# A decoder layer on one core: the gating unit's steps spread out and its operands made a step ahead, product operands built in three steps, and down-projection chunks of 5, 14, 5, 14 and 6 k-tiles

## The chip, the cores and the metric

The kernel runs on one core of a Trainium2 chip. The metric is the device time of one execution in microseconds (us). Before the change three runs took 2702.42 to 2703.47 us, with a median of 2703.02 us. Shorter is better.

## The reference

One layer of a hybrid decoder, in float32, for 512 prompt tokens and 8 sample tokens that share the weights (2048 model columns):

```python
xn = rmsnorm(x)
q, k, v, gu, gv = split(xn @ w_in)
attn = window_attention(norm(q), norm(k), v)        # window 128, sinks, ALiBi
gu = gelu(gu); gv = layernorm(gelu(gv))
sgu = gu * (tril(W_s[group]) @ gv + b[group])       # in chunks of 128 tokens
gA, gB = sigmoid(xn @ w_gate + b_gate)
x += (gA * (attn @ w_br_attn) + gB * (sgu @ w_br_gm)) @ w_out
h = conv3(rmsnorm(x) @ w_up)
x += (silu(h_gate) * h_up) @ w_down                 # 5632 = 44 x 128 inner columns
x += sigmoid(rmsnorm(x) @ w_ple_gate) * (p @ w_ple_proj)
```

It returns x, the new keys and values, the last normalised gv rows (`gp_o`, `gs_o`) and the convolution's state.

## The kernel before, in words

**The products.** Activations lie transposed, 128 columns of the model by 520 tokens in a tile. Every operand is split into a high and a low part, and a product is made of three matmuls: high by high, high by low, low by high. A *plain* product (`ntile`, `mm`, lines 364 to 384) runs over the k-tiles of one output tile n; each k-tile takes six matmuls of 260 columns, two halves of the tokens by three. A *seven-product* pair (`wpair`, line 395) makes two output tiles of two k-tiles at a time from seven products instead of eight (Strassen's scheme in Winograd's form), each of three matmuls of 260 columns. Its parts come out of four PSUM banks a, b, c, d by copies on ACT (`snap`) and by sums on DVE (`c11`, `c22`, `c12`). The seven-product form serves the gates, the up-projection and the odd chunks of the down-projection.

**The weights.** They stream from DRAM in blocks of eight 128x128 tiles. At each block's start (`block_start`, line 292) SP starts a load, ACT casts the high part of the block two ahead (`hi`, line 279), and DVE takes the rest (`lo`, line 286). Work that was put off to a block (`at_block`) is placed there as well: "snap" before the cast, "act" and "dve" between the cast and the rest, "end" behind both.

**Who sets the order.** The order on each engine is that in which the code issues its instructions, and each engine works in that order. Side work is written as generators. `ntile` and `wpair` call `next(self.fine)` once for each k-tile, and whatever the generator does up to its next `yield` is issued there; `finish_fine` issues what is left.

**The gating unit** (`gmlp`, line 1249) is such side work, under the attention branch's projection "bra" (`branch_attn`, line 730): 16 output tiles of eight k-tiles, so 128 calls. `paced` (line 736) lets three calls pass for each step of `gmlp`. The steps, in order:

1. Load the small weights, and make the masked `whl`.
2. For each of the four token groups c, one step with eight PE transposes into two PSUM banks (`g`, line 1294) and the statistics (`stats`, DVE and a power on POOL), and one step with eight normalising writes on DVE (line 1298). All `aux` tiles share four banks.
3. For each of eight column slices d, three steps: multiply by the norm's weight (line 1310), start the `gp_o` write from POOL, and split into `gnh` (ACT, line 490) and `gnl` (DVE, line 491); two calls of the generator later the mix on PE (`mx`, lines 1320 and 1321) and its sums on DVE (lines 1327 to 1330); then one more step.
4. For the samples: eight transposes, statistics, two normalised tiles `gn` and four small diagonals `dgs` (line 1344), two steps of pause, and 16 tiny matmuls `gx` (line 1351).

The 16 gelus on which all this rests (line 1256) are issued on ACT just ahead of the first step.

**The operands of the seven products** (`woperands`, line 440) are made as side work too. For each product p of a pair of k-tiles, `begin` issues the operand's own sums on DVE (none for P1, P2, P7 and P3, one for P5 and P4, two for P6) and at once the ACT cast `X` (line 462); `end`, one round later, issues the rest on DVE (line 465). `build` paces the rounds, by `every` calls each. It serves the plain gates (P5, P6, P4 and P7 of eight pairs), the output projection and "pproj" (`w_out`, line 1360; pproj is 16 output tiles of two k-tiles, each evicted by ACT at line 1427 and written to DRAM by a transfer that ACT itself starts, line 1428), and the even chunks of the down-projection.

**The down-projection** (`ffn_down`, line 1552) takes the 44 inner k-tiles in chunks of 6, 14, 6, 12 and 6 (`FF_CHUNKS`, line 49). Chunks 0 and 2 are plain; under them the operands of the next chunk are loaded from DRAM (`fr`, line 1540) and built, with one or two calls to a round by turns. Chunks 1 and 3 are made in the seven-product form; the plain operands of the chunk behind are split under their last pairs (`f_parts`). Each result but the last chunk's is added to `x1d` in DRAM by a transfer that POOL starts (line 1558). Chunk 4 is plain and adds on DVE (`down_last`).

## Time and profile before

| | before |
|---|---|
| median of 3 runs | 2703.02 us |
| the profiled execution's own time | 2702.04 us |
| its span, first to last instruction | 2700.3 us |
| PE busy | 2673.4 us (99%), 22212 matmuls |
| DVE busy | 1871.6 us (69%) |
| ACT busy | 1287.4 us (48%) |
| POOL busy | 288.4 us (11%) |
| mean granted TensorE clock | 0.998 |
| DMA moved | 438.06 MB, mean 162 GB/s |

The profile is of one execution. Engines are PE (matmuls; PEld its weight loads), DVE (VectorE), ACT (ScalarE), POOL (GpSimd) and SP, which here only starts transfers. A group of instructions is named output <- inputs, after the tiles in the code. The view of the waits gives, for each engine and line, what ended the wait, the total in us, how often, and the longest. The timeline gives start, length and, in brackets, the idle time before an instruction and its releaser. The table by stretches gives the busy time of each engine in each stretch, the granted clock and the share of time in which the 16 DMA engines were busy. A busy PE is not yet a PE at its full clock.

### The profile page before, as it was taken

The numbers are of one execution on the slowest core, as the hardware profiler recorded it, in microseconds if no ns is written. First come the engines' busy times: TensorE is split into PE (matmuls) and PEld (weight loads), VectorE is DVE, ScalarE is ACT, GpSimd is POOL, SyncE is SP. The second block draws the span as 40 slices with busy tenths as digits, with TensorE's granted clock in tenths as the row PEclk, the third lists the DMA queues.
The fourth block names the chain that finished last, engine by engine and source line by source line (L and its number), as shares of the span: only waits on it lengthen the run. The fifth ranks groups of instructions, "written<-read, shape, count | busy, mean of one in ns | idle before, by whom it ended". The sixth has DMA issues, their size and how long they took to land.

```text
span 2700.3 us, 53713 instructions
## 1 busy us (share of the span) xinstructions
PE 2673.4 (99%) x22212; PEld 2668.0 (99%) x22212; DVE 1871.6 (69%) x2791; ACT 1287.4 (48%) x2173; POOL 288.4 (11%) x443
## 2 busy tenths in 40 slices
PE   9999999999999999999999999999999999999999
PEld 9999998999999999999999999999999999999999
DVE  6666557567666533688888888888888676576533
ACT  5365452354444233555555555555556445444321
POOL 0111001000010000011111111111111111110000
PEclk9999999999999999999999999999999999999999
DMA  5223323567667444566666666666668677675333
GB/s 188 93 81 102 103 79 122 184 206 204 190 188 239 158 134 142 193 186 171 163 177 174 162 174 174 162 177 171 166 167 249 152 180 204 153 178 183 125 132 106
DMA packets 151797, 438.06 MB, mean 162 GB/s; under 512 B 17200, under 2 KB 18352, under 8 KB 151552
## 3 DMA queue, kind: packets, MB, share of 16 engines
q1 hardware_dynamic: 117504, 337.58, 37.1%
q0 software_dynamic: 29440, 88.53, 18.8%
q10 hardware_dynamic: 4608, 8.52, 0.8%
q8 instruction: 174, 2.85, 0.4%
q14 instruction: 71, 0.58, 0.1%
HBM read 373.23 MB, written 61.33 MB: 161 GB/s over the span
## 4 chain that ended last, share of the span: by engine, by line
PE 96%; DVE 2%; ACT 1%; issue 0%; DMA 0%; POOL 0%; ACTq 0%; SPq 0%; DVEq 0%; POOLq 0%
PE wa L433 22%; PE wb L433 15%; PE mm L372 14%; PE mm L376 14%; PE mm L374 14%; PE wd L433 7%; PE wc L433 7%; PE po L1106 1%; PE s L1043 1%; ACT hi L279 0%; PE pt L1088 0%; PE pl L1654 0%; DVE lo L286 0%; DVE z L1298 0%; ACT z L1256 0%
## 5 line engine op out<-in xcount | busy, mean ns | idle before, releaser
L286 DVE TENSOR_TENSOR lo<-st,hi 128x1024 fp32r<-128x1024 f32 (+3 forms) x352 | 421.9, 1198 | 268.9 <-ACT hi L279 261.3
L433 PE MATMUL wa<-X,hi 128*128 128x260 f32 x3152 | 576.6, 283 | 0.9 <-ACT pp L1427 0.9
L433 PEld LDWEIGHTS wa<-X,hi 128*128 128x128 f32 x3152 | 485.5, 188 | 1.1 <-ACT pp L1427 1.1
L279 ACT CAST hi<-st 128x1024 fp32r<-128x1024 f32 (+3 forms) x352 | 362.3, 1029 | 195.8 <-DMA st<-in_w 83.8
L433 PE MATMUL wa<-X,lo 128*128 128x260 f32 x1576 | 444.7, 282 | 0.0
L433 PE MATMUL wb<-X,hi 128*128 128x260 f32 x2032 | 371.5, 283 | 0.0
L279 ACT CAST hi<-S 128x1024 fp32r<-128x1024 f32 (+2 forms) x219 | 222.6, 1017 | 230.0 <-DVE S L312 171.7
L286 DVE TENSOR_TENSOR lo<-S,hi 128x1024 fp32r<-128x1024 f32 (+2 forms) x219 | 258.5, 1180 | 99.9 <-ACT hi L279 99.6
L433 PEld LDWEIGHTS wb<-X,hi 128*128 128x128 f32 x2032 | 312.8, 188 | 0.0
L433 PEld LDWEIGHTS wa<-X,lo 128*128 128x128 f32 x1576 | 296.7, 188 | 0.0
L433 PE MATMUL wb<-X,lo 128*128 128x260 f32 x1016 | 286.7, 282 | 0.0
L286 DVE TENSOR_TENSOR lo<-L,hi 128x1024 fp32r<-128x1024 f32 (+2 forms) x146 | 172.5, 1181 | 125.0 <-ACT hi L279 124.6
L372 PE MATMUL mm<-xn,hi 128*128 128x260 f32 x1088 | 222.9, 286 | 5.3 <-ACT hi L279 5.3
L376 PE MATMUL mm<-xn,lo 128*128 128x260 f32 x1088 | 219.6, 283 | 0.0
L374 PE MATMUL mm<-xn,hi 128*128 128x260 f32 x1088 | 219.3, 283 | 0.0
L279 ACT CAST hi<-L 128x1024 fp32r<-128x1024 f32 (+2 forms) x146 | 148.4, 1016 | 121.3 <-PE wd L433 118.8
L433 PE MATMUL wd<-X,hi 128*128 128x260 f32 x1120 | 205.1, 283 | 0.0
L310 POOL DMA_DIRECT2D L<-in_w x73 | 63.3, 867 | 1265.5 <-issue 828.9
L433 PEld LDWEIGHTS wb<-X,lo 128*128 128x128 f32 x1016 | 191.4, 188 | 0.0
L372 PEld LDWEIGHTS mm<-xn,hi 128*128 128x128 f32 x1088 | 168.4, 190 | 5.4 <-ACT hi L279 5.3
L433 PEld LDWEIGHTS wd<-X,hi 128*128 128x128 f32 x1120 | 172.2, 188 | 0.1
L376 PEld LDWEIGHTS mm<-xn,lo 128*128 128x128 f32 x1088 | 168.8, 189 | 0.0
(313 smaller groups left out, 5966.8 us busy)
## 6 DMA issues: line engine op xcount, KB each, us to landing
st<-in_w SPq DMA_DIRECT2D x317, 512.0 KB, 4.4
S<-in_w SPq DMA_DIRECT2D x57, 512.0 KB, 3.5
S<-in_w POOLq DMA_DIRECT2D x57, 512.0 KB, 7.9
L<-in_w SPq DMA_DIRECT2D x57, 512.0 KB, 4.0
L<-in_w POOLq DMA_DIRECT2D x57, 512.0 KB, 5.6
fd<-hb SPq DMA_DIRECT2D x44, 260.0 KB, 2.2
fr<-fd SPq DMA_DIRECT2D x44, 260.0 KB, 4.9
xr<-in_x SPq DMA_DIRECT2D x32, 260.0 KB, 4.2
```

Of the source, the lines that this page charges most:

```text
L279: self.nc.scalar.copy(self.hi[v][:, c], self.st[WS.src[v]][:, c])
L286: self.nc.vector.tensor_sub(self.lo[v][:, c], self.st[WS.src[v]][:, c], self.hi[v][:, c].bitcast(F32))
L310: self.nc.gpsimd.dma_start(self.st[kind, r][:, c], self.a["w"][src][:, c], accum_op=ALU.add)
L372: mm(ps[:, h, 0:HW], lhsT=whi, rhs=xh[h], start=start, stop=False)
L374: mm(ps[:, h, 0:HW], lhsT=whi, rhs=xl[h], start=False, stop=False)
L376: mm(ps[:, h, 0:HW], lhsT=wlo, rhs=xh[h], start=False, stop=stop)
L433: nc.tensor.matmul(ps(z), lhsT=w, rhs=x, start=new and i == 0 and q == 0, stop=i == len(X[p]) - 1 and q == 2, skip_group_check=True)
L1043: nc.tensor.matmul(out, lhsT=self.cols(q, c), rhs=keys(kk, c), start=n == 0, stop=n == 1)
L1106: nc.tensor.matmul(po[:, kb * 128:kb * 128 + w], lhsT=vv[:, kb * 128:(kb + 1) * 128], rhs=pp[:, o:o + w], start=kb == 0 and n == 0, stop=k ...
```

## The change

There are four edits.

- **Gating unit.** `paced` lets four calls pass for each step instead of three. Slice d's multiplication, `gp_o` write and split become `parts(d)`, its mix and sums `mix(d, h, l)`. `parts(d + 1)` is issued one step ahead of `mix(d)`, and a slice takes two steps instead of three. The samples' transposes and statistics go from behind the slices to ahead of them: the transposes stand in one step with `parts(0)`, the normalised tiles and `dgs` in the next. `gx` stays last.
- **Operands in three steps.** `steps` replaces `begin` and `end`: a round issues the rests of the items two rounds old (`lo`, DVE), the casts of those one round old (`hi`, ACT), and the own sums of the new ones (`own`, DVE).
- **The sum of bank d** leaves `c12` and becomes `c21`, which is issued with `c22` at the start of product P3's block, ahead of that block's `lo`.
- **Chunks** of 5, 14, 5, 14 and 6 k-tiles; the operands of chunks 1 and 3 are built in rounds of 1, 1, 1 and 2 calls.

```diff
-FF_CHUNKS = (6, 14, 6, 12, 6)
+FF_CHUNKS = (5, 14, 5, 14, 6)
...
+        def c21():
+            nc.vector.tensor_sub(part("c2", 0), ps("d"), part("un", 1))
+
         def c12():
             nc.vector.tensor_add(part("c1", 1), ps("b"), part("un", 0))
-            nc.vector.tensor_sub(part("c2", 0), ps("d"), part("un", 1))
...
-                 "P6": [("snap", lambda: snap("a", "un", 0))], "P7": [("snap", lambda: snap("a", "un", 1)), ("dve", c22)],
+                 "P6": [("snap", lambda: snap("a", "un", 0))], "P7": [("snap", lambda: snap("a", "un", 1)), ("dve", c22), ("dve", c21)],
...
+            def own():
+                nonlocal src
+                if p == "P5":
+                    src = self.slot(name="tau")[:, 0:HW]
+                    nc.vector.tensor_sub(src, b11, b12)
...
+            def hi():
+                nonlocal x
+                x = self.slot(F32R, "X")
+                nc.scalar.copy(x[:, 0:HW], src)
+
+            def lo():
                 nc.vector.tensor_sub(x[:, HW:NT], src, x[:, 0:HW].bitcast(F32))
                 X[p][i] = x
...
+            hi, lo = [], []
+            while items or hi or lo:
                 for _ in range(every if isinstance(every, int) else next(every)):
                     yield
-                now, items = items[:group], items[group:]
-                new = [begin(*x) for x in now]
-                for e in ends:
-                    e()
-                ends = new
+                for f in lo:
+                    f()
+                for f, _ in hi:
+                    f()
+                lo = [f for _, f in hi]
+                new = [steps(*x) for x in items[:group]]
+                items = items[group:]
+                for f, _, _ in new:
+                    f()
+                hi = [f[1:] for f in new]
...
             for _ in g3:
-                yield
-                yield
-                yield
+                yield from [None] * 4
...
+        hl = parts(0)
+        yield
         g = [self.slot(name="gn") for _ in range(2)]
...
+        for d in range(KG):
+            new = parts(d + 1) if d + 1 < KG else None
+            yield
+            mix(d, *hl)
+            hl = new
+            yield
...
-                    X, self.fine = self.down_operands(ch[c + 1], cycle((1, 2)))
+                    X, self.fine = self.down_operands(ch[c + 1], cycle((1, 1, 1, 2)))
```

On DVE in the gating unit, behind the last normalising write of the fourth group (`z` from `g`), there stands before the first slice (its product with the norm's weight `nw`, and `gnl`), then a weight block's `lo` and the first slice's sums:

```order
L1298 TENSOR_SCALAR z_3625<-g_571_5382,sm_5394,sm_5398 128x128
L1310 TENSOR_TENSOR z_1265<-z_1265,nw_5134 128x2x256
L491 TENSOR_TENSOR gnl_5457<-z_1265,gnh_5456 128x520
L286 TENSOR_TENSOR lo_5491<-st_5416,hi_5490 128x1024
L1327 TENSOR_TENSOR mx_5516<-mx_5506,bb 128x256
```

At the same place there stands now:

```order
L1307 TENSOR_SCALAR z_3625<-g_573_5434,sm_5446,sm_5450 128x128
L1319 TENSOR_TENSOR z_1265<-z_1265,nw_5134 128x2x256
L502 TENSOR_TENSOR gnl_5531<-z_1265,gnh_5530 128x520
L286 TENSOR_TENSOR lo_5559<-st_5474,hi_5558 128x1024
L1290 BN_STATS sm_5570<-g_580_5518 8x6
L1290 BN_STATS sm_5570<-g_581_5519 8x6
L1292 BN_AGGR sm_5573<-sm_5570 8x2
L1294 TENSOR_SCALAR sm_5575<-sm_5573 8x1
L1351 TENSOR_SCALAR gn_5568<-g_580_5518,sm_5573,sm_5577 8x512
L1353 TENSOR_TENSOR gn_5568<-gn_5568,nw_5134 8x512
L1351 TENSOR_SCALAR gn_5569<-g_581_5519,sm_5573,sm_5577 8x512
L1353 TENSOR_TENSOR gn_5569<-gn_5569,nw_5135 8x512
```

The samples' chain (which goes on with `dgs`) has come between the first slice's operand and its sums; the second slice's operand follows it, ahead of the first slice's sums.

On ACT in pproj, around the fourth and fifth evictions and a block's cast (`hi`), there stands before:

```order
L462 CAST X_13558<-tau_13556 128x260
L1427 COPY pp_13567<-mm_13549 128x520
L1428 DMA ppd_146<-pp_13567 128x520
L279 CAST hi_13571<-st_13489 128x1024
L462 CAST X_13583<-tau_13581 128x260
L1427 COPY pp_13592<-mm_13570 128x520
L1428 DMA ppd_147<-pp_13592 128x520
```

and now:

```order
L468 CAST X_13554<-xb_13463 128x260
L1444 COPY pp_13564<-mm_13546 128x520
L1445 DMA ppd_146<-pp_13564 128x520
L279 CAST hi_13568<-st_13489 128x1024
L468 CAST X_13579<-tau_13556 128x260
L1444 COPY pp_13589<-mm_13567 128x520
L1445 DMA ppd_147<-pp_13589 128x520
```

Each cast `X` stands one tile later than before, so that the cast behind this `hi` reads `tau_13556`, which DVE makes a round earlier, and no longer `tau_13581`.

On DVE at the end of chunk 3, the sums of banks a, d and b (`wa`, `wd`, `wb`) of the last pair stood before in this order around the weight blocks' `lo`:

```order
L414 SCALAR_TENSOR_TENSOR c_1949_29807<-wa_29635,sn_29662 128x260
L286 TENSOR_TENSOR lo_29805<-st_29773,hi_29804 128x1024
L418 TENSOR_TENSOR c_1946_29752<-wb_29661,un_29718 128x260
L419 TENSOR_TENSOR c_1949_29807<-wd_29746,un_29718 128x260
L286 TENSOR_TENSOR lo_29850<-st_29801,hi_29849 128x1024
```

and now:

```order
L414 SCALAR_TENSOR_TENSOR c_1953_29774<-wa_29585,sn_29620 128x260
L418 TENSOR_TENSOR c_1953_29774<-wd_29711,un_29680 128x260
L286 TENSOR_TENSOR lo_29772<-st_29741,hi_29771 128x1024
L421 TENSOR_TENSOR c_1952_29717<-wb_29619,un_29680 128x260
L286 TENSOR_TENSOR lo_29820<-st_29768,hi_29819 128x1024
```

The sum of bank d has moved one `lo` ahead.

## The prediction

> **What bounds the kernel now.** I read the profile's page first, then the waits of PE, then the timeline and the table by stretches at each place where PE waits. The page:

> ```profile
> span 2700.3 us, 53713 instructions
> ...
> PE 2673.4 (99%) x22212; PEld 2668.0 (99%) x22212; DVE 1871.6 (69%) x2791; ACT 1287.4 (48%) x2173; POOL 288.4 (11%) x443
> ...
> PE 96%; DVE 2%; ACT 1%; issue 0%; DMA 0%; POOL 0%; ACTq 0%; SPq 0%; DVEq 0%; POOLq 0%
> ```

> PE is the bound nearly throughout: the chain that ended last runs on it for 96% of the span. So only three things shorten the kernel: fewer matmuls, fewer waits of PE, and less time at a lowered clock. The view of PE's waits, of which these are the rows that bear on the change:

> ```profile
> PE mx L1320 <- ACT gnh L490: 3.7, 1, 3.7
> PE mm L372 <- ACT pp L1427: 2.6, 3, 1.4
> PE gx L1351 <- DVE dgs L1344: 2.2, 1, 2.2
> PE g L1294 <- DVE z L1298: 2.0, 3, 0.8
> PE mm L372 <- DVE c L418: 1.5, 2, 0.9
> ...
> PE wa L433 <- ACT pp L1427: 0.9, 1, 0.9
> ...
> PE mx L1321 <- DVE gnl L491: 0.6, 2, 0.4
> ```

> The gating unit (mx, gx, g) holds 3.7 + 0.6 + 2.2 + 2.0 = 8.5 us, pproj (pp) 3.5 us, the ends of chunks 1 and 3 (c) 1.5 us. Two of the gating unit's waits cost more than they last, as the table by short stretches shows (the granted clock stands before the last two numbers):

> ```profile
> 429.40:430.00 0.60, 0.25 (x2) 0.18 (x2) 0.37 (x1) 0.20 (x2) 0.00 (x0) 0.93 0.26 89
> 430.00:430.60 0.60, 0.60 (x4) 0.60 (x5) 0.00 (x0) 0.60 (x1) 0.00 (x0) 0.50 0.40 149
> 433.00:433.60 0.60, 0.60 (x5) 0.60 (x5) 0.56 (x3) 0.00 (x0) 0.00 (x0) 0.72 0.47 123
> 494.80:495.40 0.60, 0.60 (x5) 0.60 (x4) 0.60 (x1) 0.00 (x0) 0.00 (x0) 0.50 0.07 14
> 501.40:502.00 0.60, 0.60 (x6) 0.60 (x6) 0.00 (x0) 0.00 (x0) 0.00 (x0) 0.83 1.03 392
> ```

> From 430.0 on PE is busy in these rows, but at half its clock. The mixed rows give the ends: 0.93 leaves 0.14 of 0.6 us at half, so it began at 429.9, and 0.72 and 0.83 end it at 433.3 and 501.6. So it lasts from 429.9 to 433.3 us behind the wait of mx, and from 494.8 to 501.6 us in and behind gx.

> **The change part by part.**

> *Chunks.* Two k-tiles go from plain to seven-product chunks. Plain they take 2 x 16 output tiles x 6 = 192 matmuls, in pairs 8 x 7 x 3 = 168: 24 fewer. The chain prices them:

> ```profile
> 605.18 2.89 PE wa L433 x24
> ```

> So 24 matmuls are 2.9 us, all on the path, and **2.9 us** go. The work of DVE and ACT on the weights grows a little in chunk 3 (blocks of seven tiles for six). Its cover is PE's product, 21 x 0.12 = 2.5 us for 2.2; chunk 1 has these blocks already, without a wait inside it. If that failed, each late block would show as a wait on lo.

> *Gating unit.* Of what PE waits for here, DVE is late:

> ```profile
> 404.87 1.29 DVE L1281 BATCH_NORM_STATS2 sm<-g 128x6 f32<-128x512 f32 x2
> 421.80 1.29 DVE L1281 BATCH_NORM_STATS2 sm<-g 128x6 f32<-128x512 f32 x2
> 427.70 0.68 DVE L1310 TENSOR_TENSOR z<-z,nw 128x512 f32<-128x512 f32 x1
> 429.07 0.70 DVE L491 TENSOR_TENSOR gnl<-z,gnh 128x520 fp32r<-128x520 f32 x1 [0.69 <-ACT gnh L490]
> 431.01 1.23 DVE L286 TENSOR_TENSOR lo<-st,hi 128x1024 fp32r<-128x1024 f32 x1 [1.24 <-ACT hi L279]
> 432.15 0.42 DVE L1327 TENSOR_TENSOR mx<-mx,bb 128x256 f32<-128x256 f32 x1
> 434.46 0.69 DVE L1310 TENSOR_TENSOR z<-z,nw 128x512 f32<-128x512 f32 x1
> 488.60 1.28 DVE L1281 BATCH_NORM_STATS2 sm<-g 8x6 f32<-8x512 f32 x2
> 493.90 0.61 DVE L1344 TENSOR_SCALAR dgs<-ident,cvt 8x8 f32<-8x8 f32 x4
> ```

> A token group takes DVE 427.70 - 421.80 = 5.9 us, one block's lo included. An operand (multiply, cast, rest) takes 429.77 - 427.70 = 2.1 us, a slice's sums 434.46 - 432.15 = 2.3 us, the samples' chain 494.5 - 488.6 = 5.9 us. PE's side:

> ```profile
> 397.40 1.03 PE L1294 MATMUL g<-ident,z 128*128 128x128 f32 x8
> 438.76 0.28 PE L1320 MATMUL mx<-whl,gnh 128*128 128x256 f32 x1
> 439.63 0.45 PE L372 MATMUL mm<-ah,hi 128*128 128x260 f32 x2
> 266.95 1.85 PE L1172 MATMUL sT<-qe,kT 128*128 128x8 f32 x16
> 494.26 3.09 PE L1351 MATMUL gx<-dgs,gn 8*128 8x8 f32 x16 [2.24 <-DVE dgs L1344]
> ```

> A call is one k-tile, 6 x 0.12 = 0.72 us; a mix adds 439.63 - 438.76 = 0.9 us, and I take 0.9 for eight transposes too. Before, a group gets six calls and its transposes, 5.2 us, against DVE's 5.9, and the first slice's mix comes six calls after its operand is issued. So PE runs into DVE three times at g and once at mx. After, a group gets eight calls, 6.7 us.

> I walk the new order with these times, from DVE's first statistics at 404.87, which the gelus ahead hold, not the pace. Four groups end at 404.87 + 4 x 5.9 = 428.5, and the first operand at 430.6. PE comes to the first mix at call 49; call 4 was at 397.4, so 45 x 0.72 + 5 x 0.9 later, at 434.3: 3.7 us to spare. The second operand now stands behind a lo and the samples' chain: 430.6 + 1.2 + 5.9 + 2.1 = 439.8, against the second mix at 434.3 + 8 x 0.72 + 0.9 = 441.0: 1.2 us to spare. From there a slice costs DVE 1.2 + 2.3 + 2.1 = 5.6 us and PE 6.7, so the margin grows. The banks for the third group's transposes are free at 404.87 + 5.9 = 410.8, and PE comes at 397.4 + 17 x 0.72 + 2 x 0.9 = 411.4: 0.6 us, the smallest margin. gx comes at call 109 of 128, its inputs long done.

> So 8.5 us of waits go. With them goes the half clock: (433.3 - 429.9) / 2 = 1.7 us, and (501.6 - 494.8) / 2 = 3.4 us. Together **13.6 us**. For gx I lean on sT: 16 products as narrow took 1.85 us at full clock, so narrow products alone did not lower it there. From above, six restarts of PE at 0.1 to 0.2 us each could go as well (14.6). From below, the half clock at gx stays and margins of 0.6 and 1.2 us become waits (8.5).

> [...]

> The gp_o writes move one step earlier on POOL, behind which only the small power of a statistics step waits; POOL is 11% busy. gnh's cast now stands on ACT ahead of an eviction of bra that has 5.8 us, and two operand pairs are alive instead of one, so a cast may wait for the mix two slices back, which PE passes 2.9 us earlier. I cost both at nothing; failing that, PE would wait at mm for its eviction.

> *Operands in three steps.* ACT no longer stops for DVE's own sums. Where PE does not wait (plain gates, output projection, chunks 0 and 2) that is worth nothing, since PE's work covers it. In pproj it is worth something, for there ACT is the slowest:

> ```profile
> 1129.38 1.05 ACT L279 CAST hi<-st 128x1024 fp32r<-128x1024 f32 x1 [0.40 <-ACT pp L1427]
> 1132.05 0.41 ACT L462 CAST X<-tau 128x260 fp32r<-128x260 f32 x1 [1.63 <-DVE tau L451]
> 1132.37 0.59 ACT L1427 COPY pp<-mm 128x520 f32<-128x520 f32 x1
> ```

> The stop of 1.63 us shrinks to some 0.3, since tau was made a round ahead. Against it, the last round of the builder before pproj is one longer: two casts, 2 x 0.32 = 0.65 us, now stand ahead of the first eviction. Net **0.7 us** of the 3.5. Bounds: all 3.5 go, or 1.3 us are added (two casts more, and the writes to DRAM set the pace anyway).

> *Bank d's sum.* Each pair's c21 lies ahead of a lo that is needed two blocks (5.8 us) later, so its 0.4 us cost nothing. PE waits for bank b's sum at the ends of chunks 1 and 3, and that still stands behind a lo. Only chunk 3's longer last block helps: 0.36 us later. I take **0.3 us** of 1.5; bounds all of it, or 0.8 more.

> *Chunks 0 and 2* get shorter, from 96 to 80 calls, 69.1 to 57.6 us. A build of seven pairs is 63 rounds, 79 calls with the first: it just fits.

> ```profile
> 2050.00:2100.00 50.00, 50.00 (x419) 50.00 (x418) 38.67 (x80) 30.25 (x66) 10.93 (x13) 1.00 0.98 247
> st<-in_w SPq DMA_DIRECT2D x8, 512.0 KB, 5.1
> x1d<-dn POOLq DMA_DIRECT2D x13, 260.0 KB, 5.7
> fr<-fd SPq DMA_DIRECT2D x12, 260.0 KB, 5.8
> ```

> In chunk 0 DVE is 77% and ACT 61% busy. The operands' work, packed into 57 instead of 61 us, brings DVE to some 83%. The DMA engines are at 0.98 already. Landing times still leave room: fr is asked for 11 to 14 calls (8 to 10 us) ahead and lands in 5.8, st has two blocks (11.5 us) for 5.1. I cost it at nothing, with 4.3 us for each chunk as the upper bound (a build that keeps its 61.9 us); the 2050 row is the nearest.

> **The sum.** 13.6 + 2.9 + 0.7 + 0.3 = 17.5 us. The profiled execution took 2702.04 us, its span and 1.7 us around it; that gives 2684.5. The median was 1.0 us above that execution, so I forecast 2685.5 us.

> **The rivals.**

> *The plain chunks are held by their operands.* For it: DMA at 0.98, and rounds 1.25 calls apart. Against: no wait of PE there before, and landing times half of what is allowed. Price: up to 4.3 us in each, so 2690 to 2694. [...]

> *The gating unit's waits move more than they go.* For it: margins of 0.6 and 1.2 us, and a chain of 5.9 us put ahead of the second slice. Against: DVE needs less than PE in each step from then on. If half of 13.6 stays: 2692.

> *Slower.* Each tile of a plain chunk still takes what its six k-tiles took, 4.3 us instead of 3.6, since evictions, accumulating writes and operands behind one another are what paces it: 16 x 0.72 = 11.5 us for each chunk, 23.0 for both, against 17.5 gained: 2708.5. It decides once both chunks lose more than 8.8 us each, half the gain. Against it: landing times did not climb at 0.98.

> *It does not do what it says:* DVE's lateness comes from the gelus alone, and all of the gating unit's loss stays under other names. Then 3.9 us go: 2699.1.

> **How the numbers follow.** Forecast 0.74, operands late 0.10, waits half kept 0.09, slower 0.04, no effect 0.03. 0.2%, about what a measurement of this kernel can tell from no change, is 5.4 us. Faster by more: 0.74 + 0.10 + 0.09 = 0.93; same 0.03; slower 0.04. Range: the low end takes the gating unit at 14.6 and most of pproj's 3.5 (2682); the high end reaches over the first two rivals (2694).

> **What would show it.** Right: no wait at mx, gx or g over 0.5 us, a granted clock of 1.00 from 400 to 510 us, PE's count lower by 24, pproj's wait near 2.8 us, no wait of PE in chunks 0 and 2. Wrong: a wait at the second slice's mx, a clock of 0.5 behind gx, waits of PE on fl, lo or X at the start of chunks 1 and 3, or on dn in the plain chunks.

## The result, and the profile after

Four runs of the changed kernel took 2683.59 to 2685.71 us, with a median of 2684.86 us, against 2702.97 us for the kernel before beside them: 18.1 us less, a ratio of 0.9933 (95% interval 0.9915 to 0.995). The forecast was 2685.5 us. The profiled execution took 2685.71 us; its span is 2684.0 us, 16.3 us less than before. The total was met; two of its four terms, the chunks by themselves and the sum of bank d, were not. The page of the kernel after:

```profile
span 2684.0 us, 53655 instructions
...
PE 2665.3 (99%) x22188; PEld 2659.5 (99%) x22188; DVE 1879.6 (70%) x2796; ACT 1287.7 (48%) x2174; POOL 288.2 (11%) x443
```

PE has 24 matmuls fewer, 22188. Its waits, from the view of the waits of the kernel after:

```profile
PE mm L372 <- ACT hi L279: 5.9, 2, 5.4
PE mm L372 <- ACT pp L1444: 2.1, 4, 0.8
...
PE wa L435 <- ACT pp L1444: 0.9, 1, 0.9
...
PE wc L435 <- DVE lo L286: 0.6, 1, 0.6
PE mm L372 <- ACT dn L1598: 0.5, 1, 0.5
...
PE mm L372 <- ACT ae L755: 0.4, 1, 0.4
```

No wait at mx, gx or g is left, and none on c at the ends of chunks 1 and 3. pproj (pp) still holds 2.1 + 0.9 = 3.0 us of its 3.5. Two waits are new: 0.5 us for an eviction of the plain chunks (dn), and 0.4 us for one of bra (ae), which stands on ACT behind the second slice's cast of gnh.

In the gating unit, the timeline of the kernel after (start, length, and in brackets the idle time ahead):

```profile
406.19 1.29 DVE L1290 BATCH_NORM_STATS2 sm<-g 128x6 f32<-128x512 f32 x2
431.21 0.70 DVE L502 TENSOR_TENSOR gnl<-z,gnh 128x520 fp32r<-128x520 f32 x1 [0.69 <-ACT gnh L501]
435.51 0.28 PE L1329 MATMUL mx<-whl,gnh 128*128 128x256 f32 x1
441.50 0.70 DVE L502 TENSOR_TENSOR gnl<-z,gnh 128x520 fp32r<-128x520 f32 x1 [0.69 <-ACT gnh L501]
442.83 0.28 PE L1329 MATMUL mx<-whl,gnh 128*128 128x256 f32 x1
487.60 1.95 PE L1368 MATMUL gx<-dgs,gn 8*128 8x8 f32 x16
```

The first statistics came at 406.19 and not at 404.87, since this execution's whole stage began 1.3 us later. With that shift the walk of the prediction gives 431.9 for the first operand's end and 435.6 for the first mix; the rows show 431.9 and 435.51. The second operand ends at 442.2, 1.1 us later than walked, for a mix at 442.83: 0.6 us to spare, where 1.2 was forecast. gx runs at full clock, 1.95 us for 3.09. But a stretch at half clock follows it, as the table by short stretches shows (granted clock before the last two numbers):

```profile
489.40:490.00 0.60, 0.60 (x6) 0.58 (x6) 0.60 (x2) 0.00 (x0) 0.00 (x0) 0.93 0.00 0
490.00:490.60 0.60, 0.60 (x5) 0.60 (x5) 0.57 (x2) 0.00 (x0) 0.00 (x0) 0.50 1.48 150
...
493.00:493.60 0.60, 0.60 (x5) 0.60 (x5) 0.00 (x0) 0.17 (x1) 0.00 (x0) 0.72 1.03 388
```

By its mixed rows it lasts from 489.9 to 493.3 us and costs 1.7.

Where the 16.3 us between the two traces come from, by starts of the same instructions in both:

| stretch | before, us | after, us | less, us |
|---|---|---|---|
| start of the span to the branch projection | 393.4 | 394.8 | -1.4 |
| branch projection (first to last k-step) | 121.2 | 109.4 | 11.8 |
| gates | 423.9 | 423.8 | 0.1 |
| output projection | 182.9 | 183.8 | -0.9 |
| pproj and the norm behind it | 57.8 | 57.5 | 0.3 |
| up-projection | 859.7 | 857.3 | 2.4 |
| chunks 0 to 4 | 471.6 | 467.2 | 4.4 |
| the rest | 189.8 | 190.2 | -0.4 |

Three rows were not in the forecast: 1.4 us lost at the start, 0.9 in the output projection, and 2.4 gained in the up-projection, whose instructions the change touches only in the place of one sum.

### The profile page after: what moved, and what is told of

Read it like the earlier page. It is cut to its first block, busy times and chain, and to the rows that moved or that the text cites. A ratio compares the mean times of both kernels' runs of the same rounds, so it can differ in the third digit from the quotient of the medians.

```text
span 2684.0 us, 53655 instructions
## 1 busy us (share of the span) xinstructions
PE 2665.3 (99%) x22188; PEld 2659.5 (99%) x22188; DVE 1879.6 (70%) x2796; ACT 1287.7 (48%) x2174; POOL 288.2 (11%) x443
## 4 chain that ended last, share of the span: by engine, by line
PE 94%; DVE 2%; ACT 1%; DMA 1%; issue 1%; POOL 0%; SPq 0%; ACTq 0%; DVEq 0%; POOLq 0%
PE wa L435 22%; PE wb L435 15%; PE mm L372 13%; PE mm L376 13%; PE mm L374 13%; PE wd L435 8%; PE wc L435 8%; DMA st<-in_w 1%; PE po L1115 1%; PE s L1052 1%; DMA ppd<-pp 0%; ACT hi L279 0%; PE pt L1097 0%; PE pl L1671 0%; DVE z L1307 0%
## 5 line engine op out<-in xcount | busy, mean ns | idle before, releaser
L286 DVE TENSOR_TENSOR lo<-st,hi 128x1024 fp32r<-128x1024 f32 (+2 forms) x348 | 419.1, 1204 | 255.5 <-ACT hi L279 252.3
L435 PE MATMUL wa<-X,hi 128*128 128x260 f32 x3200 | 582.7, 283 | 0.9 <-ACT pp L1444 0.9
L279 ACT CAST hi<-st 128x1024 fp32r<-128x1024 f32 (+2 forms) x348 | 360.3, 1035 | 204.4 <-DMA st<-in_w 91.2
L279 ACT CAST hi<-S 128x1024 fp32r<-128x1024 f32 (+1 forms) x219 | 225.3, 1029 | 233.6 <-DVE S L312 173.6
L286 DVE TENSOR_TENSOR lo<-S,hi 128x1024 fp32r<-128x1024 f32 (+1 forms) x219 | 261.8, 1195 | 90.8 <-ACT hi L279 89.5
L286 DVE TENSOR_TENSOR lo<-L,hi 128x1024 fp32r<-128x1024 f32 (+1 forms) x146 | 174.6, 1196 | 123.4 <-ACT hi L279 118.2
L372 PE MATMUL mm<-xn,hi 128*128 128x260 f32 x1088 | 223.2, 286 | 5.9 <-ACT hi L279 5.9
L279 ACT CAST hi<-L 128x1024 fp32r<-128x1024 f32 (+1 forms) x146 | 150.0, 1027 | 121.2 <-PE wd L435 120.8
L372 PEld LDWEIGHTS mm<-xn,hi 128*128 128x128 f32 x1088 | 168.3, 189 | 6.2 <-ACT hi L279 6.1
L435 PE MATMUL wc<-X,hi 128*128 128x260 f32 x928 | 169.9, 284 | 0.0
## 6 DMA issues: line engine op xcount, KB each, us to landing
st<-in_w SPq DMA_DIRECT2D x313, 512.0 KB, 4.5
S<-in_w SPq DMA_DIRECT2D x57, 512.0 KB, 3.5
S<-in_w POOLq DMA_DIRECT2D x57, 512.0 KB, 7.8
L<-in_w SPq DMA_DIRECT2D x57, 512.0 KB, 4.0
L<-in_w POOLq DMA_DIRECT2D x57, 512.0 KB, 5.5
```

The lines of the kernel that those rows point to most:

```text
L279: self.nc.scalar.copy(self.hi[v][:, c], self.st[WS.src[v]][:, c])
L286: self.nc.vector.tensor_sub(self.lo[v][:, c], self.st[WS.src[v]][:, c], self.hi[v][:, c].bitcast(F32))
L372: mm(ps[:, h, 0:HW], lhsT=whi, rhs=xh[h], start=start, stop=False)
L435: nc.tensor.matmul(ps(z), lhsT=w, rhs=x, start=new and i == 0 and q == 0, stop=i == len(X[p]) - 1 and q == 2, skip_group_check=True)
```

## The experiments

**Each edit by itself.** The kernel before with only the gating unit's edits, `parts`, `mix` and the samples' chain as in the change:

```diff
-                yield
-                yield
-                yield
+                yield from [None] * 4
...
+        for d in range(KG):
+            new = parts(d + 1) if d + 1 < KG else None
+            yield
+            mix(d, *hl)
+            hl = new
+            yield
```

> The kernel before with only the gating unit's edits (four calls to a step, operands a step ahead, samples' chain early). The sum's term: 13.6 us less, so 2689.4 us against 2703.0, with no wait of PE at mx, gx or g over 0.5 us. The rival, read from the two traces: the branch stage runs 393.44 to 514.6 us before and 394.8 to 504.2 after, 11.8 us less, because one 3.4 us stretch at half clock (490.0 to 493.3) still follows gx: 2691.2, and executions with and without that stretch 1.7 us apart. If the gating unit's waits only moved, 2696 or more.

Measured: 2689.66 us against 2703.26, a ratio of 0.9951 (0.9939 to 0.9963): 13.6 us less, the sum's term. Its profile has no wait at mx, gx or g and no stretch at half clock in the branch stage, which took 107.8 us for the 121.2 before.

With only the operands in three steps (`own`, `hi`, `lo`):

```diff
-        def begin(p, i):
+        def steps(p, i):
...
-            return end
+            return own, hi, lo
```

> The kernel before with only the operands made in three steps. The sum's term: pproj's waits (2.6 + 0.9 us) fall by 0.7, so 2702.3 us against 2703.0. First rival: the output projection, which took 0.9 us longer in the trace of after than of before (first to last k-step of its products 183.8 against 182.9), pays for the added rounds: 2703.2 to 2703.9. Second rival: the two more casts ahead of pproj's first eviction cost their full 1.3 us: 2704.3.

Measured: 2702.59 us, ratio 0.9996 (0.9987 to 1.0004). That is 0.7 us less, but no change lies inside the interval.

With only the sum of bank d moved:

```diff
+        def c21():
+            nc.vector.tensor_sub(part("c2", 0), ps("d"), part("un", 1))
...
-("dve", c22)],
+("dve", c22), ("dve", c21)],
```

> The kernel before with only the sum of bank d moved to the start of P3's block. The sum's term: at most the chunk ends' waits, 0.3 of 1.5 us (a part of the 0.3 came with the chunks' size): 2702.7 to 2703.0 us against 2703.0. The rival: in the trace of after the up-projection is 2.4 us shorter than in that of before (first convolution step to first plain k-step of chunk 0: 853.8 against 856.1), spread evenly over its 44 pairs, and this sum is the one thing that the change moved there. Then 2.4 us go there and up to 1.5 at the chunk ends: 2699.1 to 2700.6, with a shorter pitch of pairs in the trace.

Measured: 2700.56 us, ratio 0.9991 (0.9982 to 0.9999): 2.7 us less, where the sum had 0.3. The interval just reaches 0.3, so the traces have to decide. The chunk ends show what changed. The timeline of the kernel before at the end of chunk 3, DVE's sums of the banks and PE's first plain matmul behind them:

```profile
2440.66 0.42 DVE L418 TENSOR_TENSOR c<-wb,un 128x260 f32<-128x260 f32 x1
2441.00 0.42 DVE L419 TENSOR_TENSOR c<-wd,un 128x260 f32<-128x260 f32 x1
...
2441.23 0.48 PE L372 MATMUL mm<-fh,hi 128*128 128x260 f32 x2 [0.93 <-DVE c L418]
```

The same place with only this sum moved:

```profile
2439.19 0.42 DVE L418 TENSOR_TENSOR c<-wd,un 128x260 f32<-128x260 f32 x1
2439.65 1.23 DVE L286 TENSOR_TENSOR lo<-st,hi 128x1024 fp32r<-128x1024 f32 x1
2440.79 0.42 DVE L421 TENSOR_TENSOR c<-wb,un 128x260 f32<-128x260 f32 x1
...
2440.24 0.40 PE L372 MATMUL mm<-fh,hi 128*128 128x260 f32 x2
```

PE now starts at 2440.24, before bank b's sum begins at 2440.79: here it does not wait for that sum at all. In the kernel before it did, as the view says: it starts at 2441.23, behind the end of bank b's sum (2441.08) and before that of bank d's (2441.42). What the edit changed is the banks that the chunk's first plain tile gets. In the built programs this tile lies in the first two of the eight PSUM banks. Before, the second of these was the last pair's bank b, and PE's first matmul waits for the sum of `wb`. With bank d's sum moved the banks are dealt out in another order: the second one is now the last pair's bank a, and the matmul waits for the sum of `wa`, which ended at 2439.3. In after the banks lie as in this run.

Both chunk ends together held 1.5 us of waits, and all of it goes. Chunks 0 to 4 took 469.3 us, 2.3 less than before: 1.9 at the two ends, by the starts of the last matmul of one chunk and the first of the next, and the rest inside the chunks. The rival's other half fell: the up-projection took 859.2 us here, 0.5 less than 859.7, so this sum is not what shortened it by 2.4 in after.

With only the chunks and their rounds:

```diff
-FF_CHUNKS = (6, 14, 6, 12, 6)
+FF_CHUNKS = (5, 14, 5, 14, 6)
...
-cycle((1, 2))
+cycle((1, 1, 1, 2))
```

> The kernel before with only the chunks of 5, 14, 5, 14 and 6 k-tiles and rounds of 1, 1, 1 and 2 calls. The sum's term: 24 matmuls, 2.9 us less: 2700.1 us against 2703.0, the waits at the chunk ends about as before (1.5 us). Rival from the traces: chunks 0 to 3 together took 4.4 us less in after, so up to 1.5 us of chunk-end waits go with the sizes alone: 2698.6. The forecast's slower rival, each plain tile at its old 4.3 us: 20.1 us more than 2700.1 or so, thus about 2723.

Measured: 2703.07 us, ratio 0.9999 (0.999 to 1.0008): nothing, although 24 matmuls are gone. Its waits of PE have a new row:

```profile
PE mm L372 <- ACT dn L1581: 3.3, 2, 1.7
```

and the timeline at the first of the two, in chunk 0, shows what it is (PE's matmul last):

```profile
2082.53 1.05 ACT L279 CAST hi<-st 128x1024 fp32r<-128x1024 f32 x1
2086.73 0.41 ACT L462 CAST X<-fr 128x260 fp32r<-128x260 f32 x1 [3.15 <-DVE fr L454]
2087.53 1.03 ACT L462 CAST X<-fr 128x260 fp32r<-128x260 f32 x3 [0.39 <-DVE fr L457]
2088.47 0.58 ACT L1581 COPY dn<-mm 128x520 f32<-128x520 f32 x1
...
2083.61 1.23 DVE L286 TENSOR_TENSOR lo<-st,hi 128x1024 fp32r<-128x1024 f32 x1 [1.32 <-ACT hi L279]
2084.75 1.08 DVE L312 TENSOR_TENSOR S<-S,st 128x896 f32<-128x896 f32 x1
...
2086.21 0.43 DVE L454 SCALAR_TENSOR_TENSOR fr<-fr 128x260 f32<-128x260 f32 x1
...
2089.10 0.51 PE L372 MATMUL mm<-fh,hi 128*128 128x260 f32 x2 [1.65 <-ACT dn L1581]
```

ACT is stopped 3.15 us at the cast of P6, for its own sums on DVE (L453 and L454), which stand behind a weight block's lo (1.23 us) and the first sum of the weights of the next chunk (S, 1.08 us). The eviction dn stands behind the cast, and PE waits for the bank: 1.65 us here, and 1.60 in chunk 2, where the stop is 3.10. In the plain chunks of the kernel before, ACT's longest stop of this kind was 1.95 us, and PE had 4.3 us for a tile, where it has 3.6 now:

```profile
2065.23 1.03 ACT L462 CAST X<-fr 128x260 fp32r<-128x260 f32 x3 [1.95 <-DVE fr L457]
```

So the longest stop has grown, and a tile covers less of it.

**Operands and chunks together**, on the kernel before (both diffs above):

> The kernel before with the operands in three steps and the new chunks together. Alone they gave 0.7 us and 0.2 us less; the sum had 0.7 and 2.9. In the trace with the chunks alone PE waits 1.65 and 1.60 us for an eviction of the plain chunks, which on ACT stands behind a cast that waits 3.15 us for its own sums on DVE. If these stops are what ate the 2.9 us, three steps give most of it back: some 3.0 to 3.6 us less than before, 2699.7 to 2700.3 against 2703.3, with that wait at 0.5 us or less. The rival, that the two edits only add: 2702.4.

Measured: 2700.66 us against 2703.06, ratio 0.9989 (0.998 to 0.9997): 2.4 us less, where the two alone gave 0.7 + 0.2. The interval, 0.8 to 5.4 us less, does not quite shut out that 0.9; the trace does. No wait at dn of 0.4 us or more is left in it. Chunks 0 to 4 took 468.3 us (2039.6 to 2507.9), against 471.5 with the chunks alone and 471.6 before: the three steps give the chunks their 3 us. The runs give 0.6 us less than the 3.0 to 3.6 expected.

**The pace.** The kernel after with three calls to a step:

```diff
-                yield from [None] * 4
+                yield from [None] * 3
```

> The kernel after with three calls to a step again instead of four, all else as after. If DVE's time per group (5.9 us) and per slice (5.6 us) against PE's is what decides, as the forecast had it: PE's share of a group falls to 5.2 us, so 2.0 us of waits at g as before, some 2.9 us at the first mix, 3.9 us at the second, behind which the samples' chain now stands, and 0.4 us at each of the six others; 11 us, with a stretch or two at half clock 13 to 15: 2696 to 2700 us against after's 2684.9. The rival, that the order alone (operands a step ahead) does it: 2685 to 2688.

Measured: 2695.11 us, ratio to before 0.9969 (0.9956 to 0.9981). Its waits of PE:

```profile
PE mx L1329 <- ACT gnh L501: 2.8, 1, 2.8
...
PE g L1303 <- DVE z L1307: 2.0, 3, 0.8
PE mx L1330 <- DVE gnl L502: 1.4, 4, 0.4
...
PE g L1344 <- DVE z L1307: 0.6, 1, 0.6
```

The waits come back, 6.8 us of the 11.2, and with them a stretch at half clock (441.5 to 444.9, 1.7 us). There is one long wait at mx, at the second mix, and not two, since the first mix was hardly late (0.35 us). The branch stage took 117.8 us, 9.9 more than in an execution of after without a stretch at half clock (107.9, below). The rival, that the order alone does it, falls.

**The step ahead.** The kernel after with each operand made in the step of its own mix:

```diff
-        hl = parts(0)
...
-            new = parts(d + 1) if d + 1 < KG else None
+            hl = parts(d)
             yield
             mix(d, *hl)
-            hl = new
```

> The kernel after, with each slice's operand made in the step of its own mix and no longer a step ahead; pace of four calls and the samples' early chain as in after. By the forecast's times, DVE ends the four groups at 428.5, the samples' chain at 434.4, a weight block's rest at 435.6 and the first operand at 437.7, and PE is at the first mix at 434.3: 3.4 us of wait there, perhaps a stretch at half clock behind it (1.7), and little at the later slices, as DVE needs 5.6 us for each and PE 6.7: 2688.3 to 2690 us. The rival, that at this pace the step ahead is worth nothing: 2684.9 to 2686.

Measured: 2690.73 us (ratio to before 0.9955, 0.9943 to 0.9968), 5.9 us above after's first median.

```profile
PE mx L1329 <- ACT gnh L501: 4.0, 1, 4.0
```

The wait at the first mix is 4.0 us for the 3.4 expected, and the clock is at half from 438.4 to 445.3 us behind its beginning. In this kernel the first operand stands on DVE behind the samples' chain; the step ahead keeps it in front of that chain. So pace and order are both needed: the pace for the groups, the step ahead for the first mix.

**The samples' chain.** The kernel after with the samples' transposes, statistics and `dgs` behind the slices again, eight calls ahead of gx:

```diff
+        hl = parts(0)
+        yield
+        for d in range(KG):
...
         banks = [self.aux("g0"), self.aux("g1")]
...
-        hl = parts(0)
-        yield
         g = [self.slot(name="gn") for _ in range(2)]
...
-        for d in range(KG):
...
+        yield
         p = self.aux("gx")
```

> The kernel after with the samples' transposes, statistics and diagonals behind the slices again, two steps (eight calls, 5.8 us) ahead of gx; all else as after. The samples' chain takes DVE 5.9 us from its statistics on, and up to 1.2 us of a weight block's rest stands in it: PE waits 0 to 1.5 us at gx. If a wait there and the narrow products after it lower the clock, one or two stretches of 3.4 us at half come on top: 2686 to 2690 us against 2684.9. The rival, that the place of the chain is worth nothing at this pace: 2684.9 within 0.5.

Measured: 2686.89 us, ratio to before 0.9937 (0.9923 to 0.995). The timeline and the short stretches:

```profile
490.44 3.04 PE L1369 MATMUL gx<-dgs,gn 8*128 8x8 f32 x16 [1.47 <-DVE dgs L1362]
```

```profile
491.00:491.60 0.60, 0.60 (x5) 0.60 (x5) 0.60 (x1) 0.00 (x0) 0.04 (x1) 0.55 0.00 0
...
497.60:498.20 0.60, 0.60 (x6) 0.60 (x5) 0.00 (x0) 0.00 (x0) 0.00 (x0) 0.76 1.02 388
```

A wait of 1.47 us, and two stretches at half clock in a row, 491.1 to 497.9. As in before, gx is slow because most of it falls into the first of them. The median is 2.0 us above after's first; 0.9 of that is the up-projection (858.1 us for 857.2, see the last section).

**gx in pieces.** The kernel after with the sixteen matmuls in four pieces, four calls apart:

```diff
+            if d % 2 and d < KG - 1:
+                yield
```

> The kernel after with the sixteen matmuls of gx (1.95 us in one piece) issued in four pieces, four calls apart. In the trace of after there is no wait at gx and yet 3.4 us at half clock follow it (490.0 to 493.3). If the narrow products themselves are what halves the clock, no stretch follows the pieces of some 0.5 us: no run shows a clock under 1.000 on account of it, and the median is some 0.9 us below that of after (2684.0), for about half of after's runs showed the stretch (1.7 us). The rival, that the stretch comes from elsewhere (chance, or what stands ahead): the same spread as after, 2684.9.

Measured: 2687.77 us, ratio to before 0.9941 (0.9929 to 0.9954). The profile shows no stretch at half clock from 484 to 500 us, and a branch stage of 108.8 us; yet the time is 2.9 us above after's. The up-projection, far behind, took 859.7 us in place of 857.3. So both kernels were run once more on one chip:

> The kernel after itself, unchanged, once more, beside the spread gx. The up-projection, whose code is the same in all kernels here, took 859.7 us in the trace of before, 857.3 in after, 859.7 with gx spread, and between 857.7 and 859.7 in the other runs (first convolution write to the first plain product of chunk 0). If this is an accident of the execution or the chip, this run shows another value than 857.3 and a median apart from 2684.9, up to 2687. If it hangs on the kernel (where its tiles lie in memory, say), it is 857.3 again within 0.2, and the median 2684.9 within 0.7.

> The kernel with gx in four pieces, unchanged, once more, on the same chip as the run of after beside it. Its branch stage was 108.8 us against after's 109.4, without a stretch at half clock, but its median came out at 2687.8, 2.9 us above after's. If that is the kernel's, the difference between the two stays at about 2.9 us and the up-projection at 859.7 us; if it was the execution or the chip, the two come out within 1 us of each other, this one lower by 0 to 0.9.

Measured: after 2683.33 us (ratio 0.9928, 0.9916 to 0.994), the spread gx 2688.71 (0.9944, 0.9932 to 0.9956). The lines of the up-projection's first and the plain chunk's first instruction, of before, after, after again, and the spread gx again (first and last start in us):

```profile
L1459 DVE TENSOR_TENSOR hb<-c,R x88: 677/683/693, 1179.2 to 2049.8; 128x512 f32<-128x512 f32 x88
L372 PE MATMUL mm<-fh,hi x576: 278/282/359, 2038.9 to 2509.9; 128*128 128x260 f32 x192
```

```profile
L1476 DVE TENSOR_TENSOR hb<-c,R x88: 676/684/692, 1169.3 to 2037.0; 128x512 f32<-128x512 f32 x88
L372 PE MATMUL mm<-fh,hi x512: 277/282/388, 2026.6 to 2493.2; 128*128 128x260 f32 x171
```

```profile
L1476 DVE TENSOR_TENSOR hb<-c,R x88: 675/683/692, 1165.9 to 2033.6; 128x512 f32<-128x512 f32 x88
L372 PE MATMUL mm<-fh,hi x512: 277/282/387, 2023.2 to 2490.2; 128*128 128x260 f32 x171
```

```profile
L1478 DVE TENSOR_TENSOR hb<-c,R x88: 676/683/694, 1167.6 to 2038.1; 128x512 f32<-128x512 f32 x88
L372 PE MATMUL mm<-fh,hi x512: 277/282/388, 2027.4 to 2494.0; 128*128 128x260 f32 x171
```

2038.9 - 1179.2 = 859.7, then 857.3, 857.3 again, and 859.8. It hangs on the kernel, not on the execution or the chip. In after's second trace gx is followed by no stretch at half clock, and the branch stage took 107.9 us (393.0 to 500.9), 13.3 less than before.

**The builder's pace.** The kernel after with rounds of one and two calls, as before the change:

```diff
-cycle((1, 1, 1, 2))
+cycle((1, 2))
```

> The kernel after with the operands of chunks 1 and 3 built in rounds of one and two calls by turns, as before the change. A build takes 63 rounds; at 1.5 calls each, 80 calls hold about 53, so ten rounds are left over and issued in one piece as chunks 1 and 3 begin: some 3 us of casts on ACT and 5 us on DVE, while the products need them one after the other, 2.5 us each. PE then waits 1 to 3 us at the start of each of the two chunks: 2687 to 2691 us. The rival, that the products' own order hides it: 2684.9 to 2686.

Measured: 2697.5 us, ratio to before 0.9982 (0.9973 to 0.9991): 12.6 above after's first median, and over both expectations. PE's waits, and ACT at the end of chunk 0:

```profile
PE wa L435 <- ACT sn L406: 10.0, 2, 8.6
```

```profile
2084.84 0.41 ACT L468 CAST X<-tau 128x260 fp32r<-128x260 f32 x1 [0.57 <-ACT X L468]
2092.94 0.41 ACT L468 CAST X<-fr 128x260 fp32r<-128x260 f32 x1 [7.68 <-DMA fr<-fd]
```

I had counted the left-over rounds' work, but not their load: the last pair's fr is asked for in the round that begins the pair ahead of it, which now stood at the chunk's end. ACT waits 7.68 us for the transfer, with the first snap (sn) of the next chunk behind it. The clock falls to half during this wait, at 2090.4 by its mean of 0.54 from 2090 to 2095 us, and stays there until 2100.7, for 3.9 us behind PE's restart at 2096.8, which costs 1.9 more:

```profile
2100.40:2101.00 0.60, 0.60 (x6) 0.60 (x5) 0.36 (x1) 0.00 (x0) 0.00 (x0) 0.77 0.28 96
```

## Why the prediction was right, point by point, and where it was not

*Gating unit, 13.6 us: right.* Alone it gave 13.6; against the trace of before the stage is 13.3 us shorter in one execution of after and 11.8 in the other. That gx runs at full clock held (1.95 us). "A granted clock of 1.00 from 400 to 510 us" did not hold in the first profile: a stretch of half clock, 1.7 us, can still follow gx, the sign of "Wrong" that names a clock of 0.5 behind gx. The walk was good to 1.1 us, at the second operand. One thing that was costed at nothing costs a little: gnh's cast ahead of an eviction of bra makes PE wait 0.4 us at mm in both traces of after and with the gating unit alone.

*Chunks, 2.9 us: right in size, wrong in its ground.* The step that failed is "I cost it at nothing": the operands' work, in the shorter chunks. I weighed it by DVE's share (83% forecast) and by landing times, and gave it a rival of up to 4.3 us a chunk. The cost is neither: it is ACT's stop behind its own sums, 1.6 us a chunk, and with the kernel before's operands it eats the whole gain (0.2 us left). With the operands in three steps a part of it is left, the waits at dn in chunk 2: 0.5 and 1.0 us in the two traces of after. So the sign of "Wrong" that names waits on dn came too, at a small size.

*Operands in three steps: the step that failed* is "Where PE does not wait (plain gates, output projection, chunks 0 and 2) that is worth nothing". It was true of before's chunks and not of the new ones, where the edit is what makes the chunks pay. Its own 0.7 us in pproj is not told from nothing. pproj's waits fell by 0.5 in both traces of after, and 1.1 us of ACT's wait for a write to DRAM is left there:

```profile
1131.81 0.59 ACT L1444 COPY pp<-mm 128x520 f32<-128x520 f32 x1 [1.13 <-DMA ppd<-pp]
```

*Bank d's sum, 0.3 us: wrong.* The step that failed is "PE waits for bank b's sum at the ends of chunks 1 and 3, and that still stands behind a lo", taken as true of the changed kernel too. PE did wait for bank b's sum before, and that sum does still stand behind a lo. But the edit deals the PSUM banks out in another order, the first plain tile no longer needs bank b, and all 1.5 us of waits go. The prediction had "all of it" as a bound, without this mechanism. Of the 2.7 us measured with the edit alone, its trace puts 2.3 in the chunks and 0.5 in the up-projection.

*The sum.* Too little for bank d by about 1.2 us, no term for the up-projection's 2.4, and against them the losses at the start and in the output projection (1.4 and 0.9) and the stretch behind gx (1.7): the errors nearly cancel. That the total came out within 0.6 us is in part luck. The second set of runs of after has a median of 2683.33 us, 19.7 less than before; its profiled execution has no such stretch and an earlier start.

*The rivals.* "Held by their operands" came true in kind, by ACT's stops and not by the DMA, at 1.6 us a chunk, and one of the change's own edits takes most of it away. That the gating unit's waits only move did not come: its edits alone gave 13.6 us. The slower case, plain tiles at their old 4.3 us, did not come, not even with the chunks alone: there the stops cost 3.3 us, about what the edit saves. The case from below, that the half clock at gx stays (3.4 us), came in part: of the two traces of after one loses 1.7 us to it and one nothing. Landing times, too, were longer where the DMA engines stood at 0.98, though no wait of PE came of it: from 2050 to 2100 us of before fr took 5.8 us (4.9 over the run) and st 5.1 (4.4).

## What to carry to other kernels

Before a stage is made shorter, list the stops of each engine that serves it, and do not take them as fixed: the longest grew from 1.95 us to 3.15 here, while a shorter tile covers less. Try the edit that shortens the stops together with the one that shortens the stage: alone, each may be worth nothing. Where a wait is for a PSUM bank, ask which tile held that bank: an edit that frees another bank earlier can deal them out in another order and take the wait away.

## What the runs showed of the hardware that was not expected

```profile
2681.20:2681.40 0.20, 0.00 (x0) 0.00 (x0) 0.00 (x0) 0.00 (x0) 0.00 (x0) 0.69 0.00 0
```

What decides whether a stretch follows gx is not shown. In six traces (both of after, gating alone, operand not ahead, pace three, builder's rounds slow) gx takes 1.92 to 1.95 us, at full clock, and PE has no wait of more than 0.12 us ahead of it; a stretch follows in the first trace of after alone. The times of after agree with a stretch in some executions: six of nine runs took 2682.7 to 2684.0 us, three 2685.7 to 2686.1. The three slower ones have a mean granted clock of 0.998 or 0.999, five of the six faster ones 1.000. Ahead of the 6.8 us at half clock with the samples' chain late PE had waited 1.47 us, with gx behind the wait. The spread gx did not settle it: its two profiles show no stretch, but its times still fall into two groups about 2 us apart (2686.3 to 2687.0, 2687.8 to 2689.7), and where its slower executions lose them stays open. Five of the six slower ones have a mean granted clock of 0.999 and the four faster ones 1.000, which hints at a stretch at half clock that no profile here shows.

**The up-projection's pitch differs between kernels, and agrees where the operands lie at the same places.** Its 7392 matmuls are the same in all kernels here; in the built programs the weights lie at the same addresses in all of them. The 56 operand tiles X come to lie elsewhere whenever an edit upstream takes tiles from the pool in another order. Kernels with the same places agree: 859.7 and 859.7 us (before, chunks alone), 858.6 and 858.6 (operands with and without the chunks), 857.3, 857.3 and 857.2 (after twice, slow rounds), 859.7 and 859.8 (spread gx twice); those with other places differ by up to 2.5 us, 0.3%, spread evenly over the pairs. That the places are the cause is argued from this, not shown by moving a tile alone. So 2.4 us of after's gain came by no edit's intent. The 0.9 us lost in the output projection repeats in the same way: it took 182.9 us before and with the chunks alone, and 183.8 in the three traces with after's places.

**The start scatters.** The branch projection began at 393.0 us in one execution of after and at 394.8 in the other, and PE was busy for 9.56 us of the first 15 in the one and for 8.64 in the other. In the later one ACT waited 1.52 us for a weight block to land (st, cast at 9.85 us), where before shows 0.87; that landings set the start is an estimate from this. Over all traces the projection began at 393.0 to 395.5. With the 1.7 us of a stretch that is most of what single runs of one kernel differ by.
